# A buffer of its own for the padded input of the convolution, and ten slots in place of eleven for the other temporaries

## The chip, the cores and the metric

The kernel runs on one core of a Trainium2 chip. The metric is the device time of one execution in microseconds (us). The engines named below are PE (TensorE, the matrix engine; PEld is its weight load), DVE (VectorE), ACT (ScalarE), POOL (GpSimd) and SP (SyncE, which mostly issues transfers). SBUF is the on-chip memory of 128 partitions that the engines work from, PSUM the small memory that PE writes its products to.

## The reference

The reference is one layer of a hybrid block in fp32: 1024 latent tokens and 256 context tokens, 1024 channels. Cut to what matters here:

```python
u  = rms_norm(x, norm_w) * (1 + scale) + shift          # latent; uc the same for the context
rkv, ga, lw, la, q, k, v, gr, ma, mb = split_cols(u @ w_in)     # and uc @ w_in
r, k, v = split(conv_centred(rkv, conv_w), 3)           # 3 taps along the tokens, zero-padded
kk = normalize(heads(k * k_k))                          # 16 heads of 64 channels
for d in (0, 1):                                        # two directions
    w = exp(-exp(-softplus(-(w0[d] + tanh(lw) @ w_up[d])) - 0.5))
    a = sigmoid(a0[d] + la @ a_up[d])
    kd = k * (1 + (a - 1) * k_a)
    S, o = rwkv7_scan(r, w, kd, v, kk, a, S0[d])        # S = S*w - (S kk) (kk a)^T + v kd^T ;  o = S r
    bonus = sum(r * kd * r_k) * v
ya = ((head_norm(o_0 + o_1) + bonuses) * silu(ga)) @ w_o
yr = retention branch of (rope(q), rope(k), v, gr)      # 4 heads, two directions, chunks of 128
x  = x + gate * ((sigmoid(ma) * ya + sigmoid(mb) * yr) @ w_out);  return rms_norm(x, final_norm_w)
```

The convolution reads each token's left and right neighbour, for context and latent tokens apart.

## The kernel before

**Stages.** In the order of the profile: norms and transposes (0 to 66 us); the preparation stage `phase1a` (66 to about 830 us), which the change touches; the RWKV scan (to about 1800); retention and the gates; the output projections (from about 2200).

**Tiling.** Channels lie on the 128 partitions, tokens along the free dimension: 1280 of them (256 context, then 1024 latent), in blocks of 256, 512 and 512. Two heads of 64 channels fill the partitions, so the preparation stage loops over eight *head pairs*. fp32 is computed from halves: weights and inputs are split into a high and a low part (`wh`, `wl`; `uh`, `ul`), and each product is three matmuls for each of eight k-tiles (L330, L331, L332 in `gemm`). So a block of 512 tokens is 24 matmuls into one PSUM bank `gm`; there are four such banks. The weights of a projection are loaded by SP, copied to `wh` by ACT (L210), and subtracted to `wl` by DVE (L211); there are two buffers of each.

**One head pair** (`stage_a`): `conv_proj` for `kc`, then for `vc` (three blocks each), then for `rc` (the latent blocks alone). Each of them takes a padded buffer `xp`, clears its edges on POOL (L396 ff.), runs the projection, copies each product from PSUM into `xp` on ACT (L402), and then computes the three taps on DVE from `xp` into the result tile: L407 (times a weight), L408 and L409 (multiply and add), for the context segment (256) and the latent one (1024). L409 is thus the last reader of `xp`. Between the projections stand the *fillers*, projections of the other branch (`rope_proj`, whose DVE rows are L758 to L761, and `gate_proj`, ACT L698 and DVE L700), which keep PE fed. The norm of `kc` gives `kk` (L438); `vc` is transposed and stored to DRAM (`vt`, L451 to L456).

**A direction** (`stage_a_dir`, twice for each pair; d0 and d1 below): PE computes the low-rank products `z` and `za` (L483, L484), ACT takes their tanh into `cs` (L507) and `av` (L510). DVE scales (L511) and scans (L513, two halves), ACT takes the exponentials `pe` (L515) and `pi` (L517). DVE forms `kd` (L521; L522 reads `kc`, in d1 as its last reader), `av` (L523), then `bk` from `av`, `kd` and `pi` (L533, L534; in d0 four rows of 1280, in d1 eight rows of 256 and 1024), `kx` (L539), and `kr` (L541, L545, which reads `rc`). `bk` and `kr` share a single buffer, and POOL stores each of them to DRAM (`bkD`, `krD`) before the other can be written. L549 adds the two directions' `kd`; L467 and the rows after it, the bonus, are run in the next pair, behind its `vc`.

**Buffers.** Almost all temporaries of this stage (`xp`, `kc`, `vc`, `rc`, `kk`, `sq`, `rn`, `cs`, `av`, `pe`, `pi`, `kd`, `kx`, `vr`, `vt`, `bon` and the halves for sums) come from `slot()`, L387 to L390: one pool of `SLOTS` = 11 tiles of 128 x 1300 fp32, each handed on when its last reader is done.

**What sets the order.** The program is written once, in the order above; the scheduler of the language then puts the instructions of each engine into a fixed list, by a model of their times and by when slots and banks come free. At run time each engine works off its list and waits for semaphores. A change of the buffers therefore changes the lists of all engines, in this stage and behind it.

Of the kernel before, what the change touches and what calls it, by code (L numbers as in the profile page):

```python
# [8 lines left out]
F32 = mybir.dt.float32  # L9
# [6 lines left out]
P = 128  # L16
# [6 lines left out]
C = 64  # L23
NU = T // C
# [21 lines left out]
SSE = 0  # L46
BNE = 0
TAIL = 0
SLOTS = 11
MF = 2.0  # L50
HEAD = 2.4
HOLD = 8.0
# [76 lines left out]
class Kern:  # L129
# [258 lines left out]
    def slot(self, name, dt=F32):  # L388
        t = self.sa.tile([P, NU * (C + 1)], dt, tag="s", name=self.nm(name), bufs=SLOTS)
        return t  # L390

    def conv_proj(self, ct, wi, lat_only, wp, gps, name):

        nc, pv = self.nc, self.pv
        xp = self.slot("xp")
        nc.gpsimd.memset(xp[:, 257:259], 0.0)  # L396
        nc.gpsimd.memset(xp[:, 1283:1284], 0.0)
        if not lat_only:
            nc.gpsimd.memset(xp[:, 0:1], 0.0)
        off = lambda t0: 1 + t0 + (2 if t0 >= CTX else 0)  # L400
        self.gemm(ct, LBLOCKS if lat_only else BLOCKS, wp, gps,
                  lambda t0, n, a: nc.scalar.copy(xp[:, off(t0):off(t0) + n], a))  # L402
        y = self.slot(name)
        w = [pv[:, PV_CV + 24 * j + wi:PV_CV + 24 * j + wi + 1] for j in range(3)]
        segs = ((258, 0, LAT),) if lat_only else ((0, 0, CTX), (258, CTX, LAT))
        for (so, do, n) in segs:
            nc.vector.tensor_scalar(y[:, do:do + n], xp[:, so + 1:so + 1 + n], w[1], None, op0=ALU.mult)  # L407
            nc.vector.scalar_tensor_tensor(y[:, do:do + n], xp[:, so:so + n], w[0], y[:, do:do + n], op0=ALU.mult, op1=ALU.add)  # L408
            nc.vector.scalar_tensor_tensor(y[:, do:do + n], xp[:, so + 2:so + 2 + n], w[2], y[:, do:do + n], op0=ALU.mult, op1=ALU.add)  # L409
        return y  # L410
# [1183 lines left out]
```

## Time and profile before

| | |
|---|---|
| median of 3 runs | 2516.76 us (2515.94 to 2517.83) |
| profiled execution | 2519.69 us |
| its span in the trace | 2517.9 us |
| mean granted clock of PE | 0.984 of full speed |
| PE / DVE / ACT / POOL busy | 2405.5 / 1662.3 / 1163.3 / 561.3 us |
| preparation stage (66 to 830 us): PE / DVE / ACT busy | 748.4 / 583.9 / 310.0 of 764 us |

Three kinds of rows are used below. A timeline row has the start, the duration, the engine, the line, the operation, output and inputs by the program's names, the shape, and in brackets the idle time ahead of it on its engine with what ended it. A row of the waits has the waiting engine, tile and line, what it waited for, the total, how often, and the longest. A window row has a stretch of the span, then busy times, the granted clock of PE, the busy share of the transfer engines and GB/s. Matmuls are pipelined, so their rows overlap: a row of 512 columns lasts 0.4 us, but the next starts 0.23 us later.

### The profile page before, as it was taken

The page shows a single profiled execution, that of the slowest core. Times are in us where ns is not written, and L with a number is a line of the kernel's source. Part 1 is how long each engine was busy: PE and PEld are TensorE (multiplying, and loading weights), DVE is VectorE, ACT ScalarE, POOL GpSimd, SP SyncE. Part 2 cuts the span into 40 slices and gives each one's busy share as a digit, 9 for nine tenths or more (in the row PEclk, how much of TensorE's full clock was granted, in tenths as well). Part 3 has the DMA queues.
Part 4 walks back from the last instruction along what each step waited for, and adds up shares of the span by engine and source line. Part 5 has one row for each costly group of instructions (what it writes and reads, how often), then busy time and mean ns, then how long its engine had stood idle before and what let it go on. Part 6 is the DMA issues. An engine that isn't in the chain of part 4 may idle for free. (4 is left out here: it accounts for less than half of the span.)

```text
span 2517.9 us, 54184 instructions
## 1 busy us (share of the span) xinstructions
PE 2405.5 (96%) x21584; PEld 1954.9 (78%) x21584; DVE 1662.3 (66%) x2882; ACT 1163.3 (46%) x2547; POOL 561.3 (22%) x688
## 2 busy tenths in 40 slices
PE   7999999999999899997999999999999998999998
PEld 4888888877888799996777777777666765678988
DVE  5497797797787243443988787883377758744644
ACT  6434344334434334345655666644355434533422
POOL 2211121111121011211222222222376434400000
PEclk9999999999999899998999999999999999999999
DMA  6144344343345525354555566554465654585642
GB/s 248 53 145 128 134 153 132 137 145 120 123 153 174 174 88 147 102 137 133 161 151 169 151 184 177 155 160 121 124 193 157 211 165 153 169 276 178 198 154 84
DMA packets 338606, 385.11 MB, mean 153 GB/s; under 512 B 86826, under 2 KB 248370, under 8 KB 334258
## 3 DMA queue, kind: packets, MB, share of 16 engines
q1 hardware_dynamic: 307314, 298.80, 39.0%
q0 software_dynamic: 10944, 55.58, 6.6%
q10 hardware_dynamic: 20096, 27.27, 3.1%
q8 instruction: 170, 2.79, 0.5%
q14 instruction: 82, 0.67, 0.1%
HBM read 264.63 MB, written 116.92 MB: 152 GB/s over the span
## 5 line engine op out<-in xcount | busy, mean ns | idle before, releaser
L330 PE MATMUL gm<-uh,wh 128*128 128x512 f32 x896 | 354.6, 396 | 16.2 <-ACT xp L402 13.7
L331 PE MATMUL gm<-ul,wh 128*128 128x512 f32 x896 | 353.8, 395 | 0.7 <-DVE ul L299 0.7
L332 PE MATMUL gm<-uh,wl 128*128 128x512 f32 x896 | 353.1, 394 | 0.0
L330 PEld LDWEIGHTS gm<-uh,wh 128*128 128x128 f32 x896 | 169.4, 189 | 51.6 <-ACT xp L402 15.0
L331 PEld LDWEIGHTS gm<-ul,wh 128*128 128x128 f32 x896 | 169.9, 190 | 38.5 <-issue 1.7
L1063 POOL TENSOR_TENSOR sp<-sv,pc 64x256 f32<-64x256 f32 x152 | 104.8, 690 | 425.1 <-DVE sv L1087 202.2
L332 PEld LDWEIGHTS gm<-uh,wl 128*128 128x128 f32 x896 | 169.8, 189 | 35.1
L556 PE MATMUL gm<-uh,wlo 128*128 128x512 f32 x416 | 170.2, 409 | 0.7 <-DVE wlo L658 0.7
L556 PE MATMUL gm<-ul,whi 128*128 128x512 f32 x416 | 170.3, 409 | 0.0
L556 PE MATMUL gm<-uh,whi 128*128 128x512 f32 x416 | 170.0, 409 | 0.0
L658 DVE TENSOR_TENSOR wlo<-wraw,whi 128x256 fp32r<-128x256 f32 x168 | 80.8, 495 | 122.0 <-ACT whi L657 117.8
L556 PE MATMUL gv<-whi,uh 128*128 128x256 f32 x512 | 148.9, 291 | 0.0
L556 PE MATMUL gv<-whi,ul 128*128 128x256 f32 x512 | 147.9, 289 | 0.0
L556 PE MATMUL gv<-wlo,uh 128*128 128x256 f32 x512 | 147.8, 289 | 0.0
L211 DVE TENSOR_TENSOR lo<-raw,hi 128x512 fp32r<-128x512 f32 x128 | 93.9, 739 | 75.0 <-ACT hi L210 74.7
L210 ACT CAST hi<-raw 128x512 fp32r<-128x512 f32 x128 | 78.4, 619 | 138.4 <-PE yr L1276 65.5
L902 DVE TENSOR_TENSOR TL<-TL,tmp 128x31 f32<-128x31 f32 (+15 forms) x310 | 133.7, 431 | 8.5
L900 DVE TENSOR_TENSOR tmp<-E,TL 128x31 f32<-128x31 f32 (+15 forms) x310 | 126.3, 407 | 8.9
L1077 ACT COPY uv<-U 64x256 f32<-64x256 f32 x160 | 58.7, 367 | 157.4 <-PE U L556 83.7
L1087 DVE TENSOR_TENSOR sv<-S,sp 64x256 f32<-64x256 f32 x144 | 60.7, 421 | 105.1 <-PE S L556 58.6
L1474 PE MATMUL ro<-s,rs 128*128 128x512 f32 x256 | 124.1, 600 | 2.6 <-DVE s L1430 2.4
L210 ACT CAST wh<-wr 128x1024 fp32r<-128x1024 f32 x56 | 58.8, 1050 | 130.8 <-PE gm L331 127.4
(298 smaller groups left out, 6406.7 us busy)
## 6 DMA issues: line engine op xcount, KB each, us to landing
wr<-in_w_in SPq DMA_DIRECT2D x56, 512.0 KB, 3.5
wraw<-in_w_in SPq DMA_DIRECT2D x84, 256.0 KB, 3.4
bkD<-bk POOLq DMA_DIRECT2D x16, 1280.0 KB, 5.6
bk<-bkD SPq DMA_DIRECT2D x80, 256.0 KB, 3.4
krD<-kr POOLq DMA_DIRECT2D x16, 1024.0 KB, 4.4
raw<-in_wr SPq DMA_DIRECT2D x64, 256.0 KB, 3.4
vtD<-vt POOLq DMA_DIRECT2D x64, 160.0 KB, 4.3
bi<-bkD SPq DMA_DIRECT2D x160, 64.0 KB, 2.5
```

The lines of the kernel that those rows point to most:

```text
L210: nc.scalar.copy(hi, src)
L211: (eng or nc.vector).tensor_tensor(lo, src, hi.bitcast(F32), op=ALU.subtract)
L330: nc.tensor.matmul(acc[:, :n], hi[:, k, :], self.hi(k, t0, n), start=(k == 0), stop=False)
L331: nc.tensor.matmul(acc[:, :n], hi[:, k, :], self.lo(k, t0, n), start=False, stop=False)
L332: nc.tensor.matmul(acc[:, :n], lo[:, k, :], self.hi(k, t0, n), start=False, stop=(k == KT - 1))
L556: return self.pin(self.nc.tensor.matmul(*a, **k))
L658: self.late(nc.vector.tensor_tensor(lo[:, j % size, k:k + 2], r, h.bitcast(F32), op=ALU.subtract), "v")
L900: self.late(nc.vector.tensor_tensor(t3, et[:, j + 1:, j:j + 1].broadcast_to([P, n, m]), tl[:, j:j + 1, 0:m].broadcast_to([P, n, m]), op=AL ...
L902: self.late(nc.vector.tensor_tensor(tl[:, j + 1:, 0:m], tl[:, j + 1:, 0:m], t3, op=ALU.subtract), "v")
L1063: nc.gpsimd.tensor_tensor(sp[ch], sv[ch, h], pcs[ch].broadcast_to([64, 4, C]), op=ALU.mult)
L1087: self.lead("v", nc.vector.tensor_tensor(new[h], ps[ch], sp[ch], op=ALU.add))
L1474: nc.tensor.matmul(po, qx[d][:, k, cols], st[:, k, :], start=(d == 1 and k == 0), stop=False)
```

## The change

`SLOTS` goes from 11 to 10, and `xp` comes from a buffer of its own, of the same size, with one instance (`bufs=1`). The total of the memory is the same. No instruction computes anything else.

```diff
-SLOTS = 11
+SLOTS = 10
 ...
     def conv_proj(self, ct, wi, lat_only, wp, gps, name):
 
         nc, pv = self.nc, self.pv
-        xp = self.slot("xp")
+        xp = self.sa.tile([P, NU * (C + 1)], F32, tag="xp", name=self.nm("xp"), bufs=1)
         nc.gpsimd.memset(xp[:, 257:259], 0.0)
         nc.gpsimd.memset(xp[:, 1283:1284], 0.0)
```

The lists of the engines change with it. The three places below are all at the passage from head pair 1 to pair 2. There `kc_182` is the new pair's `kc`, `xp_178` its padded input, `xp_183` that of the new `vc`; `bk_161`, `kd_160`, `pe_158`, `pi_159` and `z_156` belong to the second direction of pair 1; `gm_179` to `gm_181` are the products of the new `kc`, `gm_184` is the first of `vc`.

**DVE**, from the latent L407 of the new `kc` on; before:

```order
L407 TENSOR_SCALAR kc_182_2156<-xp_178_2068,pv_60 128x1024 [waits Activation_49]
L408 SCALAR_TENSOR_TENSOR kc_182_2156<-xp_178_2068,pv_60,kc_182_2156 128x256 [waits DVE_49,Pool_49]
L408 SCALAR_TENSOR_TENSOR kc_182_2156<-xp_178_2068,pv_60,kc_182_2156 128x1024 [waits DVE_49]
L409 SCALAR_TENSOR_TENSOR kc_182_2156<-xp_178_2068,pv_60,kc_182_2156 128x256 [waits DVE_49]
L409 SCALAR_TENSOR_TENSOR kc_182_2156<-xp_178_2068,pv_60,kc_182_2156 128x1024 [waits DVE_49]
L533 TENSOR_TENSOR bk_161_1882<-av_151_1845,pi_159_1875 64x4x64 [waits DMASW2_49]
L534 TENSOR_TENSOR bk_161_1882<-av_151_1845,pi_159_1875 64x4x64
L533 TENSOR_TENSOR bk_161_1882<-kd_160_1878,pi_159_1875 64x4x64
```

and in the changed kernel:

```order
L407 TENSOR_SCALAR kc_182_2156<-xp_178_2068,pv_60 128x1024
L533 TENSOR_TENSOR bk_161_1882<-kd_160_1878,pi_159_1875 64x4x64 [waits DMASW1_49]
L534 TENSOR_TENSOR bk_161_1882<-kd_160_1878,pi_159_1875 64x4x64
L533 TENSOR_TENSOR bk_161_1882<-kd_160_1878,pi_159_1875 64x16x64
L534 TENSOR_TENSOR bk_161_1882<-kd_160_1878,pi_159_1875 64x16x64
L533 TENSOR_TENSOR bk_161_1882<-av_151_1845,pi_159_1875 64x4x64 [waits DVE_49]
L534 TENSOR_TENSOR bk_161_1882<-av_151_1845,pi_159_1875 64x4x64
L533 TENSOR_TENSOR bk_161_1882<-av_151_1845,pi_159_1875 64x16x64
L534 TENSOR_TENSOR bk_161_1882<-av_151_1845,pi_159_1875 64x16x64
L408 SCALAR_TENSOR_TENSOR kc_182_2156<-xp_178_2068,pv_60,kc_182_2156 128x256 [waits DVE_49]
L408 SCALAR_TENSOR_TENSOR kc_182_2156<-xp_178_2068,pv_60,kc_182_2156 128x1024 [waits DVE_49]
L549 TENSOR_TENSOR kd_160_1878<-kd_160_1878,kd_146_1826 128x1024 [waits DVE_49]
```

The eight `bk` rows of the old pair stood behind all of the new `kc`'s taps; now they stand between the first tap (L407) and the other two (L408, L409), and L549 and a weight split (L211) come ahead of L409 as well. L409 is still the last reader of `xp_178`.

**ACT**, around the copies into `xp` (L402); before:

```order
L515 ACTIVATE pe_158_1873<-cs_150_1843 128x1300 [waits DVE_49,DMASW7_49,Activation_49,Pool_49]
L517 ACTIVATE pi_159_1875<-cs_150_1843 128x1280
L210 CAST wh36_2260<-wr36_2258 128x1024 [waits DMAHW1_49,PE_49]
L402 COPY xp_178_2068<-gm_179_2078 128x256 [waits DVE_49]
L402 COPY xp_178_2068<-gm_180_2104 128x512
L402 COPY xp_178_2068<-gm_181_2130 128x512 [waits PE_49]
L402 COPY xp_183_2163<-gm_184_2173 128x256 [waits DVE_49,PE_49]
```

and now:

```order
L210 CAST wh36_2260<-wr36_2258 128x1024 [waits DMAHW1_49,PE_49]
L402 COPY xp_178_2068<-gm_181_2130 128x512 [waits PE_49]
L515 ACTIVATE pe_158_1873<-cs_150_1843 128x1300 [waits DVE_49,Activation_49,Pool_49]
L517 ACTIVATE pi_159_1875<-cs_150_1843 128x1280
L210 CAST wh2_2420<-wr2_2418 128x1024 [waits DMAHW3_49,PE_49]
L402 COPY xp_183_2163<-gm_184_2173 128x256 [waits DVE_49,Activation_49]
```

The copies into `xp_178` stood behind the exponentials L515 and L517; the last of them now stands ahead (the other two stand further up). The first copy into `xp_183` waited for DVE before, too, but for a slot; now it is the same buffer as `xp_178`.

**PE**, around the last product `z_156`, which starts d1 on the other engines; before, inside the second block of the new `kc`:

```order
L330 MATMUL gm_180_2104<-uh3_100,wh10_2074 128x512
L331 MATMUL gm_180_2104<-ul3_108,wh10_2074 128x512
L483 MATMUL z_156_1862<-lx01_512,uph_93_1376 128x512 [waits PE_49,Activation_49]
L484 MATMUL z_156_1862<-lx01_512,upl_509 128x512
L332 MATMUL gm_180_2104<-uh3_100,wl10_2075 128x512
L330 MATMUL gm_180_2104<-uh4_101,wh10_2074 128x512
```

and now, inside its third block:

```order
L331 MATMUL gm_181_2130<-ul5_110,wh10_2074 128x512
L332 MATMUL gm_181_2130<-uh5_102,wl10_2075 128x512
L483 MATMUL za_155_1858<-lx11_514,uph_93_1376 128x512 [waits PE_49,Activation_49]
L484 MATMUL za_155_1858<-lx11_514,upl_509 128x512
L483 MATMUL z_156_1862<-lx01_512,uph_93_1376 128x512 [waits PE_49,Activation_49]
L484 MATMUL z_156_1862<-lx01_512,upl_509 128x512
L483 MATMUL za_157_1866<-lx11_514,uph_93_1376 128x512 [waits Activation_49]
L484 MATMUL za_157_1866<-lx11_514,upl_509 128x512
L330 MATMUL gm_181_2130<-uh6_103,wh10_2074 128x512
```

The projections themselves stand in the same sequence; the low-rank product stands later among them, here by some thirty matmuls.

## The prediction

> **What bounds the kernel now.** I read the page's busy shares first, then a table of stages, then what TensorE (PE) waits for inside the preparation stage, and last the single rows around each wait.
>
> The page's first part (busy us, share of the span, instructions), and its fifth part's row for the first matmul of each projection triple:
>
> ```profile
> PE 2405.5 (96%) x21584; PEld 1954.9 (78%) x21584; DVE 1662.3 (66%) x2882; ACT 1163.3 (46%) x2547; POOL 561.3 (22%) x688
> ...
> L330 PE MATMUL gm<-uh,wh 128*128 128x512 f32 x896 | 354.6, 396 | 16.2 <-ACT xp L402 13.7
> ```
>
> PE is busy for 96% of the span, so only its gaps and its clock can give time. The row says that the projections waited 13.7 us for the scalar engine's copy of a finished product into the padded input `xp`. The table of stages for the preparation stage (window: length, then busy time of PE, PEld, DVE, ACT, POOL with their instructions, granted clock, DMA share, GB/s):
>
> ```profile
> 66.00:830.00 764.00, 748.39 (x3641) 628.00 (x3640) 583.87 (x648) 310.04 (x453) 129.64 (x228) 0.99 0.40 134
> ```
>
> PE does 748.4 of 764 us here: 15.6 us are open. VectorE (DVE) does 583.9. The timeline, cut to PE rows with over 0.6 us idle ahead, shows them all (start, us, row, and in brackets the idle time and its releaser):
>
> ```profile
> 345.31 0.50 PE L330 MATMUL gm<-uh,wh 128*128 128x512 f32 x1 [1.46 <-ACT xp L402]
> ...
> 440.05 0.50 PE L330 MATMUL gm<-uh,wh 128*128 128x512 f32 x1 [2.77 <-ACT xp L402]
> ...
> 530.40 0.80 PE L330 MATMUL gm<-uh,wh 128*128 128x512 f32 x1 [5.29 <-ACT xp L402]
> ...
> 619.62 0.80 PE L330 MATMUL gm<-uh,wh 128*128 128x512 f32 x1 [4.22 <-ACT xp L402]
> ...
> 707.90 0.50 PE L330 MATMUL gm<-uh,wh 128*128 128x512 f32 x1 [1.87 <-ACT rp L751]
> ```
>
> They sum to 1.46+2.77+5.29+4.22+1.87 = 15.6 us, one at each passage from a head pair to the next, from pair 2 on. Passages 0 to 1 and 1 to 2 have none. A gap also costs clock. The windows of 2 us behind three of them (length, PE busy, granted clock, DMA):
>
> ```profile
> 440.00:442.00 2.00, 1.95 (x7) 0.87 0.50 195
> 442.00:444.00 2.00, 2.00 (x6) 0.50 0.00 0
> 444.00:446.00 2.00, 2.00 (x8) 0.78 0.16 66
> ...
> 530.00:532.00 2.00, 1.60 (x4) 0.55 0.15 61
> 532.00:534.00 2.00, 2.00 (x7) 0.59 0.19 66
> ...
> 620.00:622.00 2.00, 2.00 (x6) 0.50 0.00 0
> 622.00:624.00 2.00, 2.00 (x6) 0.50 0.16 66
> 624.00:626.00 2.00, 2.00 (x6) 0.55 0.56 238
> 626.00:628.00 2.00, 2.00 (x10) 1.00 0.70 287
> ...
> 708.00:710.00 2.00, 2.00 (x9) 1.00 0.63 160
> ```
>
> Lost are 2 x (0.13+0.50+0.22) = 1.7 us after 2.77, 2 x (0.45+0.41) = 1.7 after 5.29, and 2 x (0.50+0.50+0.45) = 2.9, with the ends of the window before some 3.1, after 4.22. After 1.87 the clock is 1.00. Together 6.5, a mean of 2.2 for a stall that takes the clock along. The passages cost 15.6+6.5 = 22 us in all.
>
> **A rule on the clock.** The Trainium skill, "TensorE: Matmul & The Clock Gate", Part 1, says that PE falls to half its clock after an idle window of about 3.4 us and needs about 3.4 us of work to come back. By it a drop costs 3.4 x 0.5 = 1.7 us, which is what two of the three drops here cost; but this trace has the half clock after 2.77 us of idling already. By the rule, four stalls would cost 4 x 1.7 = 6.8 us of clock where my sum has 8.8, and only those over 3.4 us at all.
>
> **Why PE waits there, and what the change takes away.** The passage from pair 4 to 5, a DVE row and the ACT row behind it:
>
> ```profile
> 528.45 1.49 DVE L522 SCALAR_TENSOR_TENSOR kd<-kd,kc 128x1280 f32<-128x1280 f32 x1
> ...
> 529.97 1.35 ACT L402 COPY xp<-gm 128x256 f32<-128x256 f32 x3 [0.85 <-DVE kd L522]
> ```
>
> The next pair's `xp` had got the slot of the old `kc`, whose last reader is L522 of the second direction (d1). Three finished products sat in three of the four PSUM banks of `gm` until 529.97, and PE went on at 530.40, 0.46 us after L522's end. With a buffer of its own, `xp` of kc doesn't wait for a slot. In the new order of ACT these copies stand ahead of the second direction's exponentials. So this wait goes, at all passages where it stood.
>
> **What it adds.** `xp` has one buffer now. The vc convolution's first copy, into the same buffer, must wait for DVE's last L409 of kc's convolution, which reads it. And DVE's order puts the eight `bk` rows of d1, L549 and a weight split between L407 and L409 of kc, as the rows in the section on the change show. PE can run on for the three gemms of vc and one more (four banks) and then waits for vc's first copy. Each passage is thus a race: from the last lora product `z`, which starts the DVE chain, to the gemm that needs the bank, on PE; and from L511 to kc's last L409 on DVE.
>
> The race at passage 1 to 2, worked out from rows of before (DVE, then PE):
>
> ```profile
> 249.64 0.83 DVE L511 TENSOR_SCALAR cs<-cs 128x1280 f32<-128x1280 f32 x1
> ...
> 263.79 1.67 DVE L409 SCALAR_TENSOR_TENSOR kc<-xp,pv,kc 128x256 f32<-128x256 f32 x2
> 265.61 0.42 DVE L533 TENSOR_TENSOR bk<-av,pi 64x256 f32<-64x256 f32 x1 [0.15 <-DMA krD<-kr]
> ...
> 272.30 0.36 DVE L407 TENSOR_SCALAR vc<-xp,pv 128x256 f32<-128x256 f32 x1
> 272.56 1.22 DVE L211 TENSOR_TENSOR wl<-wr,wh 128x1024 fp32r<-128x1024 f32 x1
> 273.70 0.75 DVE L407 TENSOR_SCALAR vc<-xp,pv 128x1024 f32<-128x1024 f32 x1
> 274.36 1.22 DVE L549 TENSOR_TENSOR kd<-kd,kd 128x1024 f32<-128x1024 f32 x1
> 275.50 1.67 DVE L408 SCALAR_TENSOR_TENSOR vc<-xp,pv,vc 128x256 f32<-128x256 f32 x2
> ```
> ```profile
> 245.56 0.39 PE L484 MATMUL z<-lx,upl 128*128 128x512 f32 x1
> ...
> 254.73 0.28 PE L330 MATMUL gm<-uhc,wh 128*128 128x256 f32 x1
> ...
> 274.22 0.39 PE L330 MATMUL gm<-uh,wh 128*128 128x512 f32 x1
> ```
>
> DVE before: 249.64 to 263.79+1.67 = 15.8 us. Put in between: eight bk rows, 272.30-265.61 = 6.7; the split, 273.70-272.56 = 1.1; L549, 275.50-274.36 = 1.1. Now 24.7. Ahead stands the tanh, 0.8 (z's end to L511), behind it copy and start, 0.5 (as at 529.94): 26.0. PE: vc's first gemm starts at 254.73, the fifth (which needs the bank) at 274.22, 19.5; and z's last product now stands eight matmuls ahead of vc's first gemm, in place of 8.8 us ahead: 8 x 0.23 = 1.8. So 21.3, and PE waits 26.0-21.3 = **4.7 us**, where it waited for nothing.
>
> The others in the same way, with the rows of the new order counted between the same points. The prices of what else stands there, from rows of before: a first direction from L511 to kx, 516.24-508.41 = 7.8; the four full bk rows, 522.25-516.24 = 6.0; a rope filler, four rows (L758 to L761) of 0.69, 2.7; a gemm of 256 on PE, 24 matmuls, 242.34-239.47 = 2.9; one of 512, (19.5-2.9)/3 = 5.5.
>
> ```profile
> 508.41 0.82 DVE L511 TENSOR_SCALAR cs<-cs 128x1280 f32<-128x1280 f32 x1
> ...
> 516.24 1.47 DVE L533 TENSOR_TENSOR bk<-kd,pi 64x1280 f32<-64x1280 f32 x1
> ...
> 522.25 0.83 DVE L511 TENSOR_SCALAR cs<-cs 128x1280 f32<-128x1280 f32 x1
> ```
> ```profile
> L758 DVE TENSOR_TENSOR rp<-gm,rope 128x512 f32<-128x512 f32 x32 | 22.0, 686 | 36.5 <-PE gm L332 36.4
> ```
> ```profile
> 239.47 0.28 PE L330 MATMUL gm<-uhc,wh 128*128 128x256 f32 x1
> ...
> 242.34 0.40 PE L330 MATMUL gm<-uh,wh 128*128 128x512 f32 x1
> ```
>
> - 2 to 3: 24.7, two ropes 5.4 and L467 1.2 (an STT as long as the bk rows of 1024) make 31.3, with 1.3 ahead (two tanh in a row) and 0.5 behind 33.1. PE has the gemm under way, four of 512 and one of 256, 5.7+22+2.9 = 30.6. Stall 2.5 (before 1.46).
> - 3 to 4: here z of d0 starts the race. 24.7+7.8+6.0+5.4 and a split 1.1 are 45.0, with 0.8 and 0.5 46.3. PE: seven of 512, one of 256, 1.0 of lora rows, 42.4. kr of d1 stands 6 us behind bk of d0, whose buffer's store it needs; about 0.4 more. Stall 4.3 (before 2.77).
> - 4 to 5: 46.3 again, and 1.5 for kr, 4.9 us behind bk here. PE has one gemm of 256 and 0.9 of lora rows more, 46.2. Stall 1.6 (before 5.29).
> - 5 to 6: 24.7 less a split, with 1.3 and 0.5 25.4. PE: three of 512 and two of 256 (z ends where vc begins), 22.3. Stall 3.1 (before 4.22).
> - 6 to 7: PE waits there on a rope row, which stays: 1.7 (before 1.87).
>
> The store's price is from this row of the sixth part (KB, us from issue to landing); a row of the waits on the same kind of pair (total, times, longest) shows that such waits exist now:
>
> ```profile
> bkD<-bk POOLq DMA_DIRECT2D x16, 1280.0 KB, 5.6
> ```
> ```profile
> DVE bk L533 <- DMA krD<-kr: 5.5, 5, 3.7
> ```
>
> **The sum.** Stalls 4.7+2.5+4.3+1.6+3.1+1.7 = 17.9 against 15.6: +2.3. Clock: four stalls of 2.5 and more, where there were three of 2.77 and more: 4 x 2.2 = 8.8 against 6.5, +2.3 (at 1.7 to 3.1 each +0.3 to +5.9). Together +4.6. Passage 0 to 1 stays free by some 1.5 us. The slot taken away is paid in waits of `vt`, `kx` and `cs` for stores; I take them as hidden, since PE is fed from four banks and DVE has 764-584 = 180 us open. If that cover is gone, each wait goes straight into the races above, 1 to 2 us a passage. The last pair's tail ends later, behind PE's last gemms: nothing. The later stages keep their code, yet the order moves some rows there; I take 0 with 3 us either way. The profiled execution (2519.7) would come to 2524.3; it stands 2.9 above the median of the runs, so the forecast is 2516.8+4.6 = **2521.4 us**, its own range 2514 to 2529 (six races good to about 1 us each, the clock to 3, the later stages to 3).
>
> **Rivals.**
> - *The buffer does what it was freed for.* The wait for L522 goes, and DVE, which has 180 us to spare, gets kc's convolution done before the bank is needed. All `xp` stalls and their clock go, 13.7+6.5 = 20 us: 2497; with half of it 2507. For it: four of the five PE gaps ended with an `xp` copy, and the slot's last reader stands ahead of one. Against it: the order is fixed, so DVE can't do L409 ahead of bk. The point of decision is the 4.7 us at passage 1 to 2, which would have to be 0.
> - *The stalls only change places.* Relief at 4 to 5 and 5 to 6 pays for 1 to 2 and 3 to 4: 2517, within 4. The sum is only 2.8 us of stalls away from it, and if just three stalls take the clock along, this is the result.
> - *Ten slots are too few.* The store waits named above, now ahead of L511 and L523 in DVE's order, add 1.5 us to six races: 9.0, and two more drops of the clock, 4.4, on top of 4.6: 2535. For it: stores land 4 to 6 us after issue. Against: the chain idles for z anyway at 1 to 2.
>
> **How the numbers follow.** The measurement can tell about 0.2%, 5 us. The forecast has 0.47, and its middle lies at +4.6, so half of it counts as slower (0.24) and half as the same (0.23); the buffer pays 0.15, all faster; changed places 0.15, the same; too few slots 0.23, slower. So faster 0.15, same 0.38, slower 0.47. The range 2508 to 2535 takes in half the gain of the first rival and the whole of the third.
>
> **What would show it.** Right: a PE gap of 3 to 6 us at passage 1 to 2 near 274 us, released by ACT L402, which itself waits for DVE's L409 of kc; no ACT copy waiting for L522; the gap at 4 to 5 under 3 us; 0.50 clock behind four passages. Wrong: no gap at 1 to 2 (DVE faster than counted), or PE gaps in the preparation stage that sum under 12 us, or a difference that arises after 830 us.

## The result, and the profile after

The changed kernel took 2535.5 us (median of 4 runs, 2535.1 to 2537.9) beside 2516.9 us before (4 runs): a ratio of 1.0072, 95% interval 1.0052 to 1.0091. In a later comparison with more runs on one chip it was 2533.8 (6 runs, 2527.7 to 2538.7) beside 2516.6 (29 runs, 2510.4 to 2527.9): 1.0068, 1.0048 to 1.0088. So the change costs about 17 us (12 to 22), where 4.6 was forecast (2521.4). The forecast's own range, 2514 to 2529, was missed. The wider one, 2508 to 2535, ends just at the measured time: half a microsecond below the first median, one above the second.

The page's row for the first matmul of the projections, then the row of the preparation stage in the table of stages (66 to 840 us here: length, busy time of PE, PEld, DVE, ACT, POOL, granted clock, DMA share, GB/s), both of the changed kernel:

```profile
L330 PE MATMUL gm<-uh,wh 128*128 128x512 f32 x896 | 354.6, 396 | 25.4 <-ACT xp L402 23.3
```
```profile
66.00:840.00 774.00, 749.18 (x3639) 627.97 (x3638) 584.35 (x648) 307.38 (x453) 123.89 (x220) 0.98 0.38 130
```

The work of PE and DVE in the stage is what it was (749 and 584 us), but it takes some ten microseconds more, and the wait for ACT's copies into `xp` has gone from 13.7 to 23.3 us. The timeline's PE rows with more than 0.4 us of idle time ahead:

```profile
282.62 0.79 PE L330 MATMUL gm<-uh,wh 128*128 128x512 f32 x1 [9.38 <-ACT xp L402]
...
382.12 0.50 PE L330 MATMUL gm<-uh,wh 128*128 128x512 f32 x1 [2.82 <-ACT xp L402]
...
475.50 0.80 PE L330 MATMUL gm<-uh,wh 128*128 128x512 f32 x1 [8.25 <-ACT xp L402]
...
558.27 0.50 PE L330 MATMUL gm<-uh,wh 128*128 128x512 f32 x1 [0.46 <-ACT rp L751]
...
564.46 0.50 PE L330 MATMUL gm<-uh,wh 128*128 128x512 f32 x1 [0.42 <-ACT xp L402]
...
643.04 0.50 PE L330 MATMUL gm<-uh,wh 128*128 128x512 f32 x1 [0.46 <-ACT rp L751]
...
651.23 0.50 PE L330 MATMUL gm<-uh,wh 128*128 128x512 f32 x1 [2.45 <-ACT xp L402]
...
742.50 0.47 PE L330 MATMUL gm<-uh,wh 128*128 128x512 f32 x1 [0.59 <-DVE tm L760]
```

They sum to 24.8 us, against 15.6. The waits of the changed kernel in this stage (total, times, longest) name the releaser and one more wait that the forecast didn't have in this place:

```profile
ACT xp L402 <- DVE kc L409: 50.7, 6, 13.5
...
DVE bk L533 <- DMA krD<-kr: 8.5, 2, 4.3
```

No copy into `xp` waits for L522 any more; six wait for kc's last L409. And twice DVE itself waits over 4 us, for the store of `kr`. The passage from pair 1 to pair 2 shows both (DVE, ACT, POOL):

```profile
253.04 0.83 DVE L511 TENSOR_SCALAR cs<-cs 128x1280 f32<-128x1280 f32 x1 [3.94 <-ACT cs L507]
...
264.54 1.00 DVE L407 TENSOR_SCALAR kc<-xp,pv 128x256 f32<-128x256 f32 x2
269.85 0.42 DVE L533 TENSOR_TENSOR bk<-kd,pi 64x256 f32<-64x256 f32 x1 [4.31 <-DMA krD<-kr]
...
280.43 1.68 DVE L409 SCALAR_TENSOR_TENSOR kc<-xp,pv,kc 128x256 f32<-128x256 f32 x2
```
```profile
282.19 1.35 ACT L402 COPY xp<-gm 128x256 f32<-128x256 f32 x3 [13.53 <-DVE kc L409]
```
```profile
258.77 6.84 POOL L519 COPY pc<-pe 128x20 f32<-128x20 f32 x1 [8.81 <-ACT pe L515]
265.56 0.54 POOL L547 DMA_DIRECT2D krD<-kr  x1
```

From L511 to the end of L409 are 280.43+1.68-253.04 = 29.1 us; 24.7 were counted, and of the 4.4 that are missing 4.31 are DVE's wait. `kr` was ready about 259.5, but POOL issued its store at 265.56, because a copy of 128 x 20 numbers stood ahead of it and lasted 6.84 us. At the passage 3 to 4 the same happens (POOL, then DVE):

```profile
451.75 7.25 POOL L519 COPY pc<-pe 128x20 f32<-128x20 f32 x1 [5.51 <-ACT pe L515]
458.94 0.54 POOL L547 DMA_DIRECT2D krD<-kr  x1
```
```profile
463.16 0.42 DVE L533 TENSOR_TENSOR bk<-av,pi 64x256 f32<-64x256 f32 x1 [4.24 <-DMA krD<-kr]
```

**Where the 17 us are.** The stages can be cut on PE at the first and last matmul of the projections, the last output of the scan, the last transpose of the retention stage and the last output matmul. From two profiled executions of the kernel before and three of the changed one (us):

| stage | before | before, 2nd | changed | changed, 2nd | changed, 3rd |
|---|---|---|---|---|---|
| preparation | 795.4 | 794.9 | 805.8 | 805.0 | 805.0 |
| scan | 967.5 | 974.3 | 971.3 | 966.7 | 965.8 |
| retention | 402.8 | 398.4 | 407.1 | 402.1 | 405.4 |
| output | 307.7 | 310.3 | 308.0 | 308.1 | 307.3 |
| whole execution | 2519.7 | 2523.5 | 2537.9 | 2527.7 | 2529.0 |

The preparation stage loses 9.6 to 10.9 us every time. The later stages, of which no line of code was changed, move by up to 7 us each between executions of the same kernel, and by up to 10 together; the first profile of the changed kernel had a bad one.

### The profile page after: what moved, and what is told of

It is laid out like the page before. It is cut to its first block, busy times and chain, and to the rows that moved or that the text cites. A ratio compares the mean times of both kernels' runs of the same rounds, so it can differ in the third digit from the quotient of the medians.

```text
span 2535.9 us, 54151 instructions
## 1 busy us (share of the span) xinstructions
PE 2408.6 (95%) x21584; PEld 1953.4 (77%) x21584; DVE 1664.1 (66%) x2882; ACT 1159.0 (46%) x2547; POOL 560.0 (22%) x688
## 5 line engine op out<-in xcount | busy, mean ns | idle before, releaser
L330 PE MATMUL gm<-uh,wh 128*128 128x512 f32 x896 | 354.6, 396 | 25.4 <-ACT xp L402 23.3
L211 DVE TENSOR_TENSOR lo<-raw,hi 128x512 fp32r<-128x512 f32 x128 | 93.9, 740 | 81.2 <-ACT hi L210 81.1
```

Source lines behind the costliest of these rows:

```text
L211: (eng or nc.vector).tensor_tensor(lo, src, hi.bitcast(F32), op=ALU.subtract)
L330: nc.tensor.matmul(acc[:, :n], hi[:, k, :], self.hi(k, t0, n), start=(k == 0), stop=False)
```

## The experiments

Three theories stood at the start. *The race and the held copy*: `xp` is single, so vc's first copy waits for a DVE chain that now has `bk` ahead of L409 (the forecast), and on two passages POOL's copy delays a store that this chain needs. *The lost slot*: with ten slots everything starts later, and the own buffer is harmless. *Later lists*: the rest is lost behind 830 us.

**The copy on ACT.** One edit to the changed kernel:

```diff
-        nc.gpsimd.tensor_copy(self.pc[:, p, d, :], pe3[:, :, C])
+        nc.scalar.copy(self.pc[:, p, d, :], pe3[:, :, C])
```

> The changed kernel with one edit: the small copy of 128 x 20 that POOL does from pe (L519) is done by ACT. The lists of DVE and PE stay the same, row for row. Theory A (at passages 1 to 2 and 3 to 4 POOL's copy lasted 6.84 and 7.25 us, the store of kr stood behind it in POOL's queue, and DVE waited 4.31 and 4.24 us for that store ahead of bk): both DVE waits go to under 0.5, the TensorE gaps at these passages fall from 9.38 and 8.25 to about 5 and 4, and the time by 8 to 11 us, to 2524 to 2528. Rival (the store was late for its own transfer, or POOL's rows are only drawn too long): the gaps stay over 8 us and the time at 2533 to 2538.

Measured: 2524.0 (12 runs) beside 2518.7 (29): 1.0022, 1.0005 to 1.0039. The preparation stage took 795.3 us, as before the change. PE's gaps, then the passage 1 to 2 on POOL and DVE:

```profile
278.22 0.79 PE L330 MATMUL gm<-uh,wh 128*128 128x512 f32 x1 [4.93 <-ACT xp L402]
...
377.40 0.50 PE L330 MATMUL gm<-uh,wh 128*128 128x512 f32 x1 [2.81 <-ACT xp L402]
...
466.43 0.57 PE L330 MATMUL gm<-uh,wh 128*128 128x512 f32 x1 [3.90 <-ACT xp L402]
...
642.41 0.50 PE L330 MATMUL gm<-uh,wh 128*128 128x512 f32 x1 [2.45 <-ACT xp L402]
```
```profile
259.89 0.54 POOL L547 DMA_DIRECT2D krD<-kr  x1 [9.91 <-DVE kr L545]
```
```profile
253.10 0.83 DVE L511 TENSOR_SCALAR cs<-cs 128x1280 f32<-128x1280 f32 x1 [3.96 <-ACT cs L507]
...
264.59 1.00 DVE L407 TENSOR_SCALAR kc<-xp,pv 128x256 f32<-128x256 f32 x2
265.52 0.41 DVE L533 TENSOR_TENSOR bk<-kd,pi 64x256 f32<-64x256 f32 x1
...
276.08 1.67 DVE L409 SCALAR_TENSOR_TENSOR kc<-xp,pv,kc 128x256 f32<-128x256 f32 x2
```

The store goes out at 259.89, DVE doesn't wait, and its chain is 276.08+1.67-253.10 = 24.7 us, the forecast's number. The gaps that remain, 4.93, 2.81, 3.90 and 2.45, are those of the race as it was counted (4.7, 2.5, 4.3, 3.1). The rows of DVE and PE are the same in both kernels, in the same order, and ACT only has the sixteen copies more. So the 9 us of gaps between this run and the changed kernel come from the place of the copy. It fits that the changed kernel, run again, has the long copies and the gaps again:

> The changed kernel itself, once more, beside the runs below. Theory A: the TensorE gaps of the first profile come back (9.4 at passage 1 to 2, 8.3 at 3 to 4, 2.8 and 2.5 at 2 to 3 and 5 to 6), since the held POOL copies are a matter of the lists; 2529 to 2538 us, 8 to 12 above the run with the copy on ACT. Rival (the long POOL copies are an accident of one execution): the gaps are 5 and 4 as in that run, and the time about 2524.

Measured: 2533.8 (the second comparison above); copies of 6.84 and 7.25 us, gaps of 9.39 and 8.24, 2.82 and 2.46.

**The store from another queue.** The copy stays on POOL:

```diff
-        nc.gpsimd.dma_start(self.krD[p, d], kr)
+        nc.sync.dma_start(self.krD[p, d], kr)
```

> The changed kernel with the stores of kr issued by SP in place of POOL; the small copy stays on POOL. Theory A (the long copy harms only what stands behind it in POOL's queue): copies of 6 to 7 us are still seen on POOL, but DVE's waits for the store of kr ahead of bk are under 1 us, and the gaps at 1 to 2 and 3 to 4 are 4 to 6 us as with the copy on ACT; 2521 to 2529. Rival (the store is late for the transfer itself, wherever it is issued): DVE still waits some 4 us, gaps over 8, 2530 to 2537.

Measured: 2523.0 (12 runs), 1.0027, 1.0013 to 1.0041; preparation stage 794.3 us. POOL's copy and the DVE row that had waited, then the two PE gaps:

```profile
257.97 7.19 POOL L519 COPY pc<-pe 128x20 f32<-128x20 f32 x1 [8.82 <-ACT pe L515]
```
```profile
264.67 0.41 DVE L533 TENSOR_TENSOR bk<-kd,pi 64x256 f32<-64x256 f32 x1
```
```profile
277.43 0.79 PE L330 MATMUL gm<-uh,wh 128*128 128x512 f32 x1 [4.53 <-ACT xp L402]
...
465.94 0.50 PE L330 MATMUL gm<-uh,wh 128*128 128x512 f32 x1 [3.94 <-ACT xp L402]
```

The copy is as long as ever, and harmless: what cost time was the place of the store behind it.

**Ten slots alone.**

```diff
-SLOTS = 11
+SLOTS = 10
```

> The kernel before with ten slots and nothing else: the padded input xp still comes from the slots. Theory A (the race of the single xp buffer, with the held POOL copy on top, costs the time): no copy of xp waits for L409 of the new kc any more; the first copies wait for a slot, as before, for L522 of the second direction; TensorE gaps in the preparation stage 10 to 20 us in sum, none of 8 us behind a wait for L409; 2512 to 2526 us. Rival B (the lost slot alone costs the time, the own buffer is harmless): 2531 to 2540, as with both parts of the change.

Measured: 2531.5 (6 runs), 1.0043, 1.0026 to 1.0060; preparation stage 806.1 us. This missed the first theory's 2512 to 2526 and met the second's time. The gaps of over 1.2 us and ACT's waits:

```profile
260.68 0.50 PE L330 MATMUL gm<-uh,wh 128*128 128x512 f32 x1 [4.09 <-ACT xp L402]
...
352.46 0.76 PE L330 MATMUL gm<-uh,wh 128*128 128x512 f32 x1 [4.04 <-DVE tm L760]
...
537.88 0.79 PE L330 MATMUL gm<-uh,wh 128*128 128x512 f32 x1 [7.37 <-ACT xp L402]
...
630.58 0.80 PE L330 MATMUL gm<-uh,wh 128*128 128x512 f32 x1 [7.50 <-ACT xp L402]
...
723.11 0.50 PE L330 MATMUL gm<-uh,wh 128*128 128x512 f32 x1 [1.30 <-ACT xp L402]
```
```profile
ACT xp L402 <- DVE bk L534: 26.9, 5, 6.7
...
ACT xp L402 <- DVE kd L522: 25.5, 7, 5.5
```

The loss of the stage is the same 10 us, but at other passages and behind other rows: here the copies wait for a slot, from L522 or from the last `bk` row. So the lost slot is enough to cost ten microseconds; giving `xp` its own buffer moves the waits and doesn't bring the loss back. What the own buffer would cost or bring with eleven slots stays open: the two together need 79.1 KB for each partition where 75.2 are free.

**A slot's worth of relief.** `kx` uses 256 of its 1300 columns. A tile of its own of 1 KB takes one temporary out of the slots, in the changed kernel and in the one before:

```diff
-        kx = self.slot("kx")
+        kx = self.sa.tile([P, CTX], F32, tag="kx", name=self.nm("kx"), bufs=1)
```

> The changed kernel with kx in a tile of 1 KB of its own. The last low-rank product of the second direction then stands 11.5 us of PE work ahead of the first vc gemm at passage 1 to 2, in place of 1.8, while xp stays single. Theory A (the race is lost because the product stands late; with the start earlier the same DVE chain of 25 us arrives in time): no gap at 1 to 2, some 3 us at 3 to 4, all gaps under 9 us; 2508 to 2523. Rival C (the single buffer itself costs it, whenever the chain starts): gaps of 5 us and more at 1 to 2 and 3 to 4, 2530 or more.

Measured in the changed kernel: 2523.4 (12 runs), 1.0015, 1.0005 to 1.0025; preparation stage 800.2 us, 5 less than without. Neither theory was met in full: the time is just above the first one's range and well below the second's, the gap at passage 3 to 4 is 5.96 us where some 3 were expected, and one of 3.25 us stayed at passage 1 to 2, where none was expected:

```profile
276.42 0.79 PE L330 MATMUL gm<-uh,wh 128*128 128x512 f32 x1 [3.25 <-ACT xp L402]
```
```profile
232.65 0.83 DVE L511 TENSOR_SCALAR cs<-cs 128x1280 f32<-128x1280 f32 x1 [0.43 <-ACT cs L507]
...
274.63 1.27 DVE L409 SCALAR_TENSOR_TENSOR kc<-xp,pv,kc 128x1024 f32<-128x1024 f32 x1
```

With d1's product early, the chain simply begins one direction further up: 43.2 us from d0's L511 to L409, of which DVE waited some 3 us for ACT. So here DVE's rows of both directions stand in the race.

> The kernel before (eleven slots, xp from the slots) with kx, which uses 256 of 1300 columns, in a tile of 1 KB of its own, so that the slots serve one temporary less. Theory A (slots set how early the low-rank product of the second direction and the copies into xp can stand): gaps of 3 to 10 us in sum in the preparation stage where there were 15.6; 2505 to 2516. Rival (slots don't matter, the gaps come from DVE's sum of work): 2515 to 2520.

Measured in the kernel before: 2522.4 (12 runs), 1.0013, 1.0000 to 1.0026, preparation stage 798.4: not faster, as neither theory had it, and 3 us worse in the stage. Five of POOL's copies lasted 6.8 us in it, where the kernel before has three. The two edits together:

> The changed kernel with kx in its own 1 KB tile and the small copy on ACT. Theory A: of the gaps of the run with the tile alone (21.7 us in sum) the one behind a copy of 9.0 us on POOL, 3.95 at passage 5 to 6, shrinks to under 1.5, and the sum to 12 to 19; 2514 to 2522. Rival (POOL plays no part there): as that run, 2521 to 2526.

> The kernel before with both edits (kx in its own tile, the small copy on ACT). With the tile alone five copies on POOL lasted 6.8 us each, one of them ahead of a DVE wait of 4.60 us. Theory A: these waits go, the gaps of 18.3 us in sum fall to 12 to 17, 2512 to 2519 us, the fastest of these kernels or equal to the kernel before. Rival: no change, 2520 to 2524.

Measured: on the changed kernel 2520.5 (12 runs), 1.0012, 1.0001 to 1.0023, and on the one before 2520.4 (12 runs), 1.0016, 1.0003 to 1.0028. The first has the shortest preparation stage of all, 788.1 us, 7 less than before the change: gaps of 1.46, 5.51 and 2.63 are left of those over 1.2 us, and the one at passage 5 to 6 is gone, as expected. The second stands at 795.4; its five gaps fell to 15.7 us, as expected, but the time met the rival's range (2520 to 2524). Neither beats the kernel before, though the stage would let one of them.

**The later stages.** A control that moves the lists behind 830 us in about as many rows, with the preparation stage nearly as it was: the copy on ACT in the kernel before.

> The kernel before with the small copy on ACT and nothing else: a control for the stages behind 830 us, whose lists move by this edit in about as many rows (DVE: 248) as by the change (250), while the preparation stage keeps its chains of work. Theory A': any reshuffle of the later lists costs some us there, because the kernel before happens to have good ones; preparation stage within 2 us of before, whole time 2519 to 2526. Rival A'': the later loss belongs to the changed buffers; whole time within 3 us of before.

Measured: 2519.8 (11 runs) beside 2518.4 (21), 1.0010, 1.0000 to 1.0020; preparation stage 793.7. Both ranges hold this time, so the run doesn't decide between them: it leaves 0 to 5 us. Its lists behind 830 us are nearly those of the changed kernel (some 20 rows of DVE stand elsewhere). And two more profiled executions:

> The kernel before, a second profiled execution. Gaps of the preparation stage as in the first (1.5, 2.8, 5.3, 4.2, 1.9 us, to 0.1), since they follow from the lists; the scan and the retention stage differ from the first execution by up to 6 us each, with the number of clock drops. If the later stages repeat to 1 us, the spread between executions has another place.

> The changed kernel, a third profiled execution. Gaps of 9.4, 2.8, 8.3, 2.5 us in the preparation stage as twice before; scan and retention stage anywhere between the two earlier executions (971 and 967, 407 and 402 us) if their loss is clock drops by chance, or at the higher values if the lists fix it.

Measured: the gaps of over 1 us in the preparation stage repeat to 0.02 us in both kernels. The kernel before: 2517.0 (8 runs), ratio 0.9992, 0.9982 to 1.0002; the changed one: 2530.3 (2 runs), 1.0047, 1.0029 to 1.0066. The later stages are in the table above; the scan alone went from 967.5 to 974.3 between two executions of one kernel. Summing (1 - granted clock), times PE's busy time, over windows of 4 us, the scan lost 11.9 us to the clock in the first of them and 20.7 in the second. What such a loss looks like, the same wait for a load in the scan, before and in the first profile of the changed kernel, with the window behind each:

```profile
1615.25 0.96 PE L556 MATMUL B<-kt,bi 64*64 64x64 f32 x22 [1.00 <-DMA bi<-bkD]
```
```profile
1616.00:1620.00 4.00, 4.00 (x67) 1.00 0.50 126
```
```profile
1625.82 1.24 PE L556 MATMUL B<-kt,bi 64*64 64x64 f32 x28 [2.12 <-DMA bi<-bkD]
```
```profile
1626.00:1630.00 4.00, 4.00 (x35) 0.50 0.54 154
```

One microsecond more of waiting, and PE ran at half its clock for the next 4 us.

## Why the prediction was right, and where it was wrong

**What held.** The direction. That the wider range reached the measured time is luck: it went so far up only to take in the rival of too few slots, while the sum gave 4.6 us of 17. The wait for L522 went away. The race is where it was said to be, its last row is kc's L409, and the DVE chain of 24.7 us at passage 1 to 2 was met to 0.1 us once POOL was out of the way. The relief at passage 4 to 5 came (5.29 to 0.46 and 0.42), even better than the 1.6 that were counted. Passage 2 to 3 is 2.82 (2.5 forecast), 5 to 6 is 0.46 and 2.45 (3.1), 6 to 7 is 0.59 (1.7; PE waits there for DVE's rope row L760 now, and no longer for ACT's L751). The gap at passage 1 to 2 stands where it was said, but it is 9.38 us long, not 3 to 6.

**The term that was mis-sized: stalls 17.9, measured 24.8.** The failing step is the counting of the DVE chains at passages 1 to 2 and 3 to 4 as rows without waits. The forecast asked whether `kr` would find its buffer's store done (0.4 and 1.5 us at 3 to 4 and 4 to 5) but not when POOL, which issues the stores, would get to them. It counted what DVE does and what PE does, and took POOL's queue to be free. POOL's copy held the store back for 6.0 and 5.3 us at two passages, DVE waited 4.31 and 4.24, and the gaps came to 9.38 and 8.25 in place of 4.7 and 4.3. The run with the copy on ACT shows this alone. The price could have been read in the trace of before: three of its sixteen copies last over 6 us, at 342.5, 437.8 and 706.5 us. There they harmed little: with the copy on ACT in the kernel before, the five gaps stay the same to 0.1 us (1.41, 2.74, 5.26, 4.19 and 1.97).

**The clock.** +2.3 forecast, some +0.4 to +2.1 measured in the stage (6.0 and 5.0 us lost in the two profiles before; 7.1, 6.4 and 6.4 in the three of the changed kernel; summed as for the scan above). Two long stalls and two of about 2.6 cost the clock little more than the three of before. The step that scaled the loss with the number of stalls was too high, and a stall of this length doesn't always cost clock: 0.50 was granted behind the gap of 2.45 us at passage 5 to 6 in the first profile (653 to 655 us), and 1.00 behind the 2.46 of the other two.

**The rest.** "The later stages keep their code, yet the order moves some rows there; I take 0 with 3 us either way." The stage explains about 10 of 17 us. Some 7 (2 to 12) lie behind it, and a difference behind 830 us was one of the forecast's own signs of being wrong. Where it arises remains open. In the profiled executions the three later stages together are 1686, 1677 and 1679 us in the changed kernel, and 1678 and 1683 before, no difference beyond the spread.

The new lists alone don't explain it either. Behind the preparation stage, DVE and ACT have the same rows in the same order in five kernels here. The table takes the difference of the stage from the difference of the whole time (us, against the kernel before; each stage from its profiles, each result good to 3 to 5 us):

| kernel with these later lists | whole | stage | rest |
|---|---|---|---|
| changed | 17 | 10 | 7 |
| changed, copy on ACT | 5 | 0 | 5 |
| before, ten slots | 11 | 11 | 0 |
| before, `kx` in its own tile | 3 | 3 | 0 |
| before, `kx` in its own tile and copy on ACT | 4 | 0 | 4 |

So these lists cost some 3 us on the mean, which the forecast's allowance covers, and two of the five kernels lose nothing by them. The store on SP, and the changed kernel with both edits, have later lists of their own, and their rest is 8 and 10 us.

What is seen over all runs is the clock: a mean of 0.983 for the changed kernel (12 runs), 0.985 for the one before (79 runs), and within the kernel before 0.001 of mean clock goes with 1.2 to 2.2 us of time, by the comparison. But a good half of this drop belongs to the preparation stage, where PE stands at half its clock during the long gaps: there (1 - granted clock) sums to 6.8 us before and to 10.2 to 11.9 in the changed kernel, idle time included. And the runs with the copy on ACT have 0.985, as the kernel before has beside them, and are 5 us slower all the same. So the clock is at most a part of the 7 us, and that is a correlation.

**The rivals.** "Ten slots are too few" gave 2535, almost the measured time, by waits for stores ahead of L511 and L523. DVE has none there: its waits for stores are those at `bk` and `kr`. ACT's tanh into `cs`, ahead of L511, does wait for the store of `vt`, five times and 12.9 us in all; at passage 1 to 2:

```profile
246.88 1.05 ACT L507 ACTIVATE cs<-z,ph 128x256 f32<-128x256 f32 x2 [4.76 <-DMA vtD<-vt]
```

But PE's last product `z` of this direction ended at 252.18 there, and L511 started at 253.04, 0.9 us behind it, as the forecast counted (0.8). So at this passage that wait didn't set the start of the race; whether it made the scheduler place `z` later isn't shown. That the lost slot costs about 10 us by itself is nevertheless what the run with ten slots showed. "The buffer does what it was freed for" fell at its own point of decision: the 4.7 us at passage 1 to 2 weren't 0. "The stalls only change places" is what is left of the stage when POOL's copy is taken out: 795.3 us, the time of before.

## What to carry to other kernels

When a buffer is taken out of a shared pool, follow every queue that the new order runs through, the one that issues the stores too: two of the three big terms here were found by walking DVE and PE, the third stood in POOL's list. A tiny instruction on an engine that also issues transfers can hold a whole chain; look for outliers among the durations of one line (0.2 to 7.4 us for the same copy in the kernel before) before taking its mean or its busy share. And when an edit reorders stages that it doesn't touch, compare stages, and several executions, before explaining the whole difference by the place that was changed.

## What was not expected of the hardware

POOL's copy of 128 x 20 numbers lasts 0.2 to 1.5 us in most places and 3 to 9 us in some, and those of over 6 us repeat at the same passages in every profile of a kernel (6.84, 6.84 and 6.85; 7.25 three times). A long one ends when DVE stops running row into row. In the kernel before, POOL and then DVE:

```profile
437.80 6.80 POOL L519 COPY pc<-pe 128x20 f32<-128x20 f32 x1 [5.57 <-ACT pe L515]
```
```profile
443.52 1.00 DVE L407 TENSOR_SCALAR kc<-xp,pv 128x256 f32<-128x256 f32 x2
444.74 1.68 DVE L408 SCALAR_TENSOR_TENSOR kc<-xp,pv,kc 128x256 f32<-128x256 f32 x2 [0.22 <-POOL xp L399]
```

The copy ends at 444.60, just behind L407's end at 444.52, where DVE had to wait, for POOL itself. In the changed kernel it ends at 265.61, and DVE's L407 at 265.54, ahead of the wait for the store. All the copies of over 3 us in these runs end within 0.1 us of a point where DVE's rows don't overlap, or of the end of a row behind which one reads PSUM. The Trainium skill, "SBUF — State Buffer", section "SBUF: two separate sides", says that DVE and GpSimd share a pair of ports as an exclusive lock, taken for one instruction: by a DVE instruction in a 2-port perf mode, or by one with two SBUF inputs against a GpSimd instruction that reads SBUF. The trace agrees with a lock; but here the copies of over 6 us stayed out through six to ten DVE rows, and not through one alone. Rows with one input (L521, L407) are among them; whether those run in a 2-port mode the trace doesn't say. Why other copies got in between two such rows within 0.9 us isn't explained by these runs.
